# Own buffers for the merged branches, one more pair by seven products, and a reordered opening in a two-layer hybrid encoder

## The chip, the cores and the metric

The kernel runs on one core of one Trainium2 chip. The metric is the device time of one execution in microseconds (us). A core has five engines that run side by side and wait for one another through semaphores: TensorE (PE; its weight loads are listed apart as PEld), VectorE (DVE), ScalarE (ACT), GpSimd (POOL) and SyncE (SP). SP here only issues transfers; ACT and POOL issue a few too. Each engine takes its instructions strictly in the order in which they were laid down.

## What is computed

Two layers over 512 positions of width 1024. Each layer normalizes x, projects it, runs four token mixers side by side, gates and sums them, projects the sum back onto x, and then adds a gated feed-forward:

```python
for l in range(DEPTH):                        # DEPTH = 2
    h = rmsnorm(x, ln_mix[l])
    z = h @ w_in[l]
    (c_q, c_kv, k_rope, fnet_in, dq, dk, dv,
     hq, hi, hf_fwd, hf_bwd, hg, gate_logits) = split_cols(z, IN_WIDTHS)
    ...                                       # o_mla, o_fnet, o_diff, o_hgrn: 512 x 256 each
    merged = jnp.zeros_like(x)
    for n, o_branch in enumerate((o_mla, o_fnet, o_diff, o_hgrn)):
        gate = jax.nn.sigmoid(gate_logits[..., n * D_MODEL:(n + 1) * D_MODEL])
        merged = merged + gate * (o_branch @ w_branch[l, n])
    x = x + merged @ w_out[l]
    h2 = rmsnorm(x, ln_ffn[l])
    g_part, u_part = jnp.split(h2 @ w_gate_up[l], 2, axis=-1)
    x = x + (jax.nn.silu(g_part) * u_part) @ w_down[l]
```

D_MODEL is 1024 and the feed-forward is 2816 wide, which makes 22 blocks of 128.

## The kernel before

x is held transposed, as 8 tiles of 128 features by 512 positions (x[0] to x[7], 256 KB each). Every matrix operand is split into a rounded high part and a remainder: ACT writes the high part (L121, or L125 with a gain), DVE subtracts it to get the low part (L122, L126). A product of two such operands is three matmuls (`mm3`, L140 to L143). A `gemm` (L201) makes one 128 x 512 output tile from 8 blocks of 128, so from 24 matmuls. `weight` (L128) loads a 128 x 1024 block of weights over SP, and ACT and DVE split it; there are two raw buffers and three pairs of split ones (WR and WL, L30). Its instructions get a priority that moves them AHEAD = 156 places forward.

The order within each engine comes from a scheduler that works through the program by priority and puts a later instruction in front where an engine would otherwise stand idle by the scheduler's own idea of time. Buffers come from pools; a tile that reuses memory waits for the last reader of the tile that lay there.

**Opening of layer 0** (L77 to L98, L226 to L250). POOL builds the identity matrix, DVE fills `ones` and `blk64` with constants, ACT copies `blk64` (L86) and then loads the table for logarithm and exponential (L230) and issues the load of the small parameters `pk` (L231). SP issues the first quarter of the first weight block w_z[0], then x[0], the rest of that block, x[1] to x[7], and then the other weight blocks. `prenorm` (L168) multiplies each x[k] by its gain and splits it into hh[k] and hl[k], and adds up the squares of all eight tiles in `ss`. Four projections named hf00, hf01, hq0 and hg0 use this x that is not yet divided by its norm. `scale` (L186) sums `ss` over the partitions with a matmul by `ones` into `ssx` and makes the reciprocal root r; `normed` (L193) then writes hh and hl again, with r multiplied in. Everything later, first the projection `hi` (`gemm_tok`, L209), reads these.

**Mixers.** Five streams of work (HGRN, its projections, a chain of the others, gates and branches) are interleaved by a string written out by hand (ORDER, L34). The last mixer is `diff`, whose pool df is open from L852 until its generator ends. `branch` (L342) multiplies mixer output by w_branch and adds it, gated, to acc[nt]. `merged` (L371) scales each finished acc[k] by one half and splits it into mh[k] and ml[k]. These take the buffers of the tags hh and hl in pool hp, 8 of each, that hold the split x until then.

**Output projection** (L1009 to L1014). Eight gemms o0 to o7 over mh and ml; each result is added to x[nt]. Each of them reads all of mh and ml.

**Feed-forward** (L1020 to L1194). `prenorm` splits x again into hh and hl, in the same eight buffers. Three raw gemms fr0 to fr2 use it, with `scale` after the first, then `normed`. The 22 blocks are then made one pair (gate and up) at a time, as the string SEVEN says. `eight` (L1150) makes a pair by two ordinary gemms, 48 matmuls of 512 columns. `seven` (L1119) makes it by seven products of half-size blocks after Strassen and Winograd, 84 matmuls of 256 columns; two of the products are left to be run inside the next pair (`finish`, L1140). `sums` (L1069) loads what a pair by seven needs: the raw block, the wide block s31 of 1024 columns (a load over SP, and a second one from POOL that is added to it in flight), the block a22, two sums on DVE (s24), and five splits. It needs sums of x halves too, `right_sums` (L1041), which are made after pairs 0 to 3. SEVEN has six pairs by `eight` first, then 16 by `seven`. After 8, 16 and 22 pairs the down projection of these pairs is added to x.

Of the kernel before, what the change touches and what calls it, by code (L numbers as in the profile page):

```python
# [11 lines left out]
F32 = mybir.dt.float32  # L12
F32R = mybir.dt.float32r
# [6 lines left out]
P = 128  # L20
S = 512
NT = S // P
D = 1024
KD = D // P
# [4 lines left out]
LOG_EXP = "natural_log_exp_and_others"  # L29
WL, WR = 3, 2  # L30
LAYERS = range(L)
SEVEN = "8888887777777777777777"
AHEAD = 156
ORDER = "ccbccchhhchhcbchcghcchcchzccczccbccccccchgcgccchbbbcbhcgbzcbbcbccbgghcbgcgcbcccghchghchzhbccccbccccgcccccczhgcgbgchcgcccccccggggggbgcggggbcbbggcbbcbhcccbccbccccccccccccccccccbchccgbgggbchcbbbbbbhbbb"  # L34
PE = 8
PM = 4
# [10 lines left out]
PK_N = 416  # L47
# [15 lines left out]
def body(tc, io):  # L63
    nc = tc.nc
    V, A, T = nc.vector, nc.scalar, nc.tensor

    def pool(name, bufs=1, **kw):
        return tc.tile_pool(name=name, bufs=bufs, reuse_waits="tile", **kw)


    with pool("const") as cl, pool("hp") as hp, pool("wp", WL) as wp, pool("vals", side="right") as cp, \
# [2 lines left out]
            pool("pq", 2, space=bass.MemoryType.PSUM) as pq:  # L74


        ident = cl.tile([P, P], F32, name="ident")  # L77
        make_identity(nc, ident)
        ones = cl.tile([P, P], F32, name="ones")
        V.memset(ones, 1.0)  # L80
        blk64 = cp.tile([P, P], F32, name="blk64")
        V.memset(blk64, 0.0)
        V.memset(blk64[0:64, 0:64], 1.0)
# [5 lines left out]
        xpool = [None]  # L89
        x = []  # L90

        def load_x(src, who):
            xpool[0] = pool(f"x{who}", side="right")
            px = xpool[0].__enter__()
            x[:] = [px.tile([P, S], F32, name=f"x{who}_{k}") for k in range(KD)]
            return [lambda k=k: nc.sync.dma_start(x[k], src[k]) for k in range(KD)]

        def drop_x():  # L98
            xpool[0].__exit__(None, None, None)
# [5 lines left out]
        def acc_psum(name="g"):  # L105
            return pm.tile([P, S], F32, tag="mm", name=name)
# [10 lines left out]
        def add(out, a, b):  # L117
            V.tensor_tensor(out, a, b, op=ALU.add)  # L118

        def split(hi, lo, src):  # L120
            A.activation(hi, src, AF.Copy)  # L121
            V.tensor_tensor(lo, src, hi.bitcast(F32), op=ALU.subtract)  # L122

        def split_g(hi, lo, src, g):
            A.activation(hi, src, AF.Copy, scale=g)  # L125
            V.scalar_tensor_tensor(lo, src, g, hi.bitcast(F32), op0=ALU.mult, op1=ALU.subtract)  # L126

        def weight(src, n, name, cuts=(), between=None):  # L128
            raw = rp.tile([P, 1024], F32, tag="wr", name=f"wr_{name}")
            hi = wp.tile([P, 1024], F32R, tag="wh", name=f"wh_{name}")  # L130
            lo = wp.tile([P, 1024], F32R, tag="wl", name=f"wl_{name}")
            with tc.high_priority(AHEAD):
                for a, b in zip((0,) + cuts, cuts + (n,)):
                    nc.sync.dma_start(raw[:, a:b], src[:, a:b])
                    split(hi[:, a:b], lo[:, a:b], raw[:, a:b])
                    if between:
                        between.pop()()
            return hi, lo

        def mm3(ps, lh, ll, rh, rl, first, last):  # L140
            T.matmul(ps, lh, rh, start=first, stop=False)  # L141
            T.matmul(ps, lh, rl, start=False, stop=False)  # L142
            T.matmul(ps, ll, rh, start=False, stop=last)  # L143
# [57 lines left out]
        def gemm(w, hh, hl, name, ready=None):  # L201
            hi, lo = ready or weight(w, 1024, name)
            ps = acc_psum(name)
            for k in range(KD):
                c = slice(k * P, (k + 1) * P)
                mm3(ps, hi[:, c], lo[:, c], hh[k], hl[k], k == 0, k == KD - 1)
            return ps
# [18 lines left out]
        xs = nc.dram_tensor("x_mid", (KD, P, S), F32).ap()  # L226
        for l in LAYERS:
            lam_init = 0.8 - 0.6 * math.exp(-0.3 * l)
            pk = cp.tile([P, PK_N], F32, tag="pk", name=f"pk{l}")
            tc.keep_in_program_order(nc.scalar.preload_act_table_set(LOG_EXP))  # L230
            nc.scalar.dma_start(pk, io["pk"][l])  # L231


            if l == LAYERS[0]:
                with tc.high_priority(1000):
                    loads = load_x(io["x"], "in")
                    w0 = weight(io["w_z"][l, 0], 1024, "hf00", (256,), [loads[1], loads[0]])
                    for load in loads[2:]:
                        load()
            else:  # L240
                w0 = weight(io["w_z"][l, 0], 1024, "hf00")
            with pool(f"mo{l}") as mo, pool(f"mx{l}") as mp:
                hh, hl, scale, normed = prenorm(pk[:, PK_MIX:PK_MIX + 8], f"m{l}")
                first = [gemm(None, hh, hl, "hf00", w0)]
                r = scale()
                for c, name in ((1, "hf01"), (4, "hq0"), (6, "hg0")):
                    first.append(gemm(io["w_z"][l, c], hh, hl, name))
                sig0 = mp.tile([P, 3, S], F32, name="sig0")
                for j in range(2):
                    mul(sig0[:, j], first[j], r)  # L250
# [63 lines left out]
                done = set()  # L314
# [51 lines left out]
                        yield gate(n, nt)  # L366
                    done.add("gates")

                mh, ml = [], []

                def merged(n):  # L371
                    for k in range(len(mh), n):
                        h = hp.tile([P, S], F32R, tag="hh", name=f"mh{k}", bufs=KD)
                        lo = hp.tile([P, S], F32R, tag="hl", name=f"ml{k}", bufs=KD)
                        split_g(h, lo, acc[k], 0.5)
                        mh.append(h)
                        ml.append(lo)
# [472 lines left out]
                def diff():  # L850
                    yield 3
                    with pool(f"df{l}") as dp, ps_pool(f"dp{l}", 2) as dps:  # L852
# [112 lines left out]
                        for n, (i, t) in enumerate(units):  # L965
# [5 lines left out]
                            if t == NT - 1:  # L971
                                yield f"b{2 * KD - 1}"
                                yield from normed(i)
                        done.add(2)

                def chain(*gens):
                    for g in gens:
# [25 lines left out]
                for _ in hgrn_z(0):  # L1003
                    pass
                issue({"h": hgrn(), "z": hgrn_z(1), "c": chain(hgrn_v(), fnet(), mla(), diff()),
                       "g": gates(), "b": branches()}, ORDER)

# [4 lines left out]
                for nt in range(KD):  # L1012
                    ps = gemm(io["w_o"][l, nt], mh, ml, f"o{nt}", wo.get(nt))
                    add(x[nt], x[nt], ps)  # L1014

# [2 lines left out]
            with pool(f"fa{l}") as fa, pool(f"ff{l}") as fp, ps_pool(f"fr{l}", 2) as fr:  # L1020
                tc.keep_in_program_order(nc.scalar.preload_act_table_set(LOG_EXP))
                hh, hl, scale, _ = prenorm(pk[:, PK_FFN:PK_FFN + 8], f"f{l}")
# [46 lines left out]
                def sums(j):  # L1069
# [3 lines left out]
                    src = io["w_gu"][l, j]  # L1073
                    with tc.high_priority(AHEAD):
                        raw = rp.tile([P, 1024], F32, tag="wr", name=f"wr_f{j}")
# [97 lines left out]
                raw = []  # L1173
# [5 lines left out]
                for k0 in range(0, KF, 8):  # L1179
                    m = min(8, KF - k0)  # L1180
                    for j in range(k0, k0 + m):
                        (seven if SEVEN[j] == "7" else eight)(j)
                        if j < Q:
                            right_sums(j, r)
                    rest()
                    for nt in range(KD):
                        ps = acc_psum(f"d{nt}")
                        hi, lo = weight(io["w_d"][l, nt, :, k0 * P:(k0 + m) * P], m * P, f"d{nt}")
                        for j in range(m):
                            c = slice(j * P, (j + 1) * P)  # L1190
# [49 lines left out]
def layout(inp):  # L1240
# [9 lines left out]
    def tiles(a, n):  # L1250
# [18 lines left out]
    gu = gu.transpose(0, 2, 3, 1, 4).reshape(L, KF, P, 4, D // 2)  # L1269
    o["w_gu"] = np.stack([gu[:, j][:, :, [1, 0, 2, 3] if SEVEN[j] == "7" else [0, 1, 2, 3]]  # L1270
                          for j in range(KF)], 1).reshape(L, KF, P, 2 * D)
# [41 lines left out]
```

## Time and profile before

| | us |
|---|---|
| three runs | 1723.2, 1725.94, 1726.93 |
| median | 1725.94 |
| the profiled execution | 1724.95 |
| its span, first to last instruction | 1723.2 |
| what lies around the span | 1.75 |

| engine | busy us | share of the span |
|---|---|---|
| PE | 1697.8 | 99% |
| PEld | 1422.5 | 83% |
| DVE | 1179.0 | 68% |
| ACT | 808.8 | 47% |
| POOL | 43.0 | 2% |

In a row of the timeline stand the start, the time that the instruction took, engine, line and operation, the tile written and the tiles read, and in brackets how long the engine had stood idle and what ended that. A row of the chain of waits has start, time and what the time went to; there the time of a matmul is the step to the next one. A row of the busy time by stretch has, for each engine, the busy time and the number of instructions. A matmul of 512 columns is listed with 0.39 us though the next one starts 0.23 us later, since matmuls overlap, so a PE that is listed as busy may still be losing time.

### The profile page before, as it was taken

The numbers are of one execution on the slowest core, as the hardware profiler recorded it, in microseconds if no ns is written. First come the engines' busy times: TensorE is split into PE (matmuls) and PEld (weight loads), VectorE is DVE, ScalarE is ACT, GpSimd is POOL, SyncE is SP. The second block draws the span as 40 slices with busy tenths as digits, with TensorE's granted clock in tenths as the row PEclk, the third lists the DMA queues.
The fourth block names the chain that finished last, engine by engine and source line by source line (L and its number), as shares of the span: only waits on it lengthen the run. The fifth ranks groups of instructions, "written<-read, shape, count | busy, mean of one in ns | idle before, by whom it ended". The sixth has DMA issues, their size and how long they took to land.

```text
span 1723.2 us, 25722 instructions
## 1 busy us (share of the span) xinstructions
PE 1697.8 (99%) x10220; PEld 1422.5 (83%) x10220; DVE 1179.0 (68%) x1979; ACT 808.8 (47%) x1352; POOL 43.0 (2%) x68
## 2 busy tenths in 40 slices
PE   8999999999999999999999999999999999999999
PEld 6787778877787989989887777788777788899897
DVE  8858775457769647748677687754667695487473
ACT  7374353456555424525453743534564453254251
POOL 1000000000000000000000000000000000000000
PEclk9999999999999999999999999999999999999999
DMA  5222203332262435644442221142323624365443
GB/s 193 64 80 86 74 26 115 105 99 86 87 201 100 138 110 161 170 122 126 133 136 58 87 74 62 43 119 97 110 75 111 189 87 140 118 177 145 127 115 104
DMA packets 62473, 191.58 MB, mean 111 GB/s; under 512 B 7953, under 2 KB 9361, under 8 KB 62353
## 3 DMA queue, kind: packets, MB, share of 16 engines
q1 hardware_dynamic: 56304, 170.10, 30.4%
q0 software_dynamic: 5760, 19.42, 6.2%
q8 instruction: 80, 1.31, 0.3%
q10 hardware_dynamic: 288, 0.43, 0.1%
q14 instruction: 41, 0.33, 0.1%
HBM read 179.42 MB, written 4.19 MB: 107 GB/s over the span
## 4 chain that ended last, share of the span: by engine, by line
PE 87%; DVE 7%; ACT 3%; DMA 2%; issue 1%; SPq 0%; POOLq 0%; ACTq 0%; DVEq 0%
PE fb L1066 8%; PE g L142 6%; PE g L141 6%; PE g L143 6%; PE fc L1066 5%; PE fa L1066 5%; PE d L141 5%; PE d L143 5%; PE d L142 5%; PE f L142 3%; PE f L141 3%; PE f L143 3%; DMA s_f<-in_w_gu 2%; PE av L942 1%; PE sm L909 1%; PE hf L142 1%
## 5 line engine op out<-in xcount | busy, mean ns | idle before, releaser
L141 PE MATMUL g<-hhm,wh_g 128*128 128x512 f32 x512 | 202.0, 394 | 0.0
L143 PE MATMUL g<-hhm,wl_g 128*128 128x512 f32 x512 | 201.5, 394 | 0.0
L142 PE MATMUL g<-hlm,wh_g 128*128 128x512 f32 x512 | 201.5, 394 | 0.0
L143 PE MATMUL d<-ah,wl_d 128*128 128x512 f32 x352 | 136.9, 390 | 0.5 <-DVE wl_d L122 0.5
L141 PE MATMUL d<-ah,wh_d 128*128 128x512 f32 x352 | 137.2, 392 | 0.0
L142 PE MATMUL d<-al,wh_d 128*128 128x512 f32 x352 | 137.1, 390 | 0.0
L122 DVE TENSOR_TENSOR wl_g<-wr_g,wh_g 128x1024 fp32r<-128x1024 f32 x64 | 78.3, 1223 | 73.8 <-ACT wh_g L121 73.8
L121 ACT ACTIVATE wh_g<-wr_g 128x1024 fp32r<-128x1024 f32 x64 | 67.7, 1058 | 115.4 <-PE g L142 80.1
L142 PEld LDWEIGHTS g<-hlm,wh_g 128*128 128x128 f32 x512 | 96.3, 188 | 20.4 <-issue 1.5
L141 PEld LDWEIGHTS g<-hhm,wh_g 128*128 128x128 f32 x512 | 96.3, 188 | 20.2 <-issue 0.8
L143 PEld LDWEIGHTS g<-hhm,wl_g 128*128 128x128 f32 x512 | 96.3, 188 | 20.0 <-issue 0.8
L121 ACT ACTIVATE wh_d<-wr_d 128x1024 fp32r<-128x1024 f32 (+1 forms) x48 | 47.5, 989 | 111.7 <-PE d L142 85.5
L118 DVE TENSOR_TENSOR xm<-xm,d 128x512 f32<-128x512 f32 x48 | 33.0, 688 | 88.9 <-PE d L143 88.8
L121 ACT ACTIVATE wh_f<-wr_f 128x1024 fp32r<-128x1024 f32 x50 | 53.0, 1059 | 79.1 <-PE d L142 35.0
L121 ACT ACTIVATE vh_f<-s_f 128x512 fp32r<-128x512 f32 x64 | 40.1, 630 | 103.4 <-PE fb L1066 63.8
L910 DVE TENSOR_REDUCE nm<-sm 128x1 f32<-128x512 f32 x64 | 43.8, 689 | 51.3 <-PE sm L909 50.9
L143 PEld LDWEIGHTS d<-ah,wl_d 128*128 128x128 f32 x352 | 66.1, 188 | 14.9 <-DVE wl_d L122 1.4
L141 PEld LDWEIGHTS d<-ah,wh_d 128*128 128x128 f32 x352 | 66.0, 188 | 14.9 <-ACT ah L121 1.9
L142 PEld LDWEIGHTS d<-al,wh_d 128*128 128x128 f32 x352 | 66.1, 188 | 14.0 <-DVE al L122 1.2
L1066 PE MATMUL fb<-th,vh_f 128*128 128x256 f32 x256 | 75.7, 296 | 0.4 <-DVE uu L118 0.3
L1066 PE MATMUL fa<-hhf,wl_f 128*128 128x256 f32 x256 | 72.7, 284 | 0.0
L1066 PE MATMUL fa<-hlf,wh_f 128*128 128x256 f32 x256 | 72.5, 283 | 0.0
(444 smaller groups left out, 4845.6 us busy)
## 6 DMA issues: line engine op xcount, KB each, us to landing
wr_g<-in_w_g SPq DMA_DIRECT2D x64, 512.0 KB, 3.6
wr_f<-in_w_gu SPq DMA_DIRECT2D x50, 512.0 KB, 3.5
s_f<-in_w_gu SPq DMA_DIRECT2D x32, 512.0 KB, 4.5
s_f<-in_w_gu POOLq DMA_DIRECT2D x32, 512.0 KB, 5.4
wr_d<-in_w_d SPq DMA_DIRECT2D x32, 512.0 KB, 3.5
wr_b<-in_w_b SPq DMA_DIRECT2D x16, 512.0 KB, 3.4
wr_o<-in_w_o SPq DMA_DIRECT2D x16, 512.0 KB, 3.5
a_f<-in_w_gu SPq DMA_DIRECT2D x32, 256.0 KB, 3.0
```

Source lines behind the costliest of these rows:

```text
L118: V.tensor_tensor(out, a, b, op=ALU.add)
L121: A.activation(hi, src, AF.Copy)
L122: V.tensor_tensor(lo, src, hi.bitcast(F32), op=ALU.subtract)
L141: T.matmul(ps, lh, rh, start=first, stop=False)
L142: T.matmul(ps, lh, rl, start=False, stop=False)
L143: T.matmul(ps, ll, rh, start=False, stop=last)
L909: T.matmul(ps, qs[0:96, t * P:(t + 1) * P], ks[0:96], start=True, stop=True)
L910: V.tensor_reduce(nm[:, j:j + 1], ps, axis=AX.X, op=ALU.max, negate=True)
L942: T.matmul(av[e * 64:e * 64 + 64], vv[:, b, 2 * i + e], pts[i][e][:, b].rearrange("p t q -> p (t q)"), start=t == 1 and b == 0, stop=b == ...
L1066: T.matmul(ps[:, :H], lh[:, c], rh, start=first and k == 0 and n == 0, stop=k == Q - 1 and n == 2, skip_group_check=True)
```

## The change

1. **Merged branches.** mh and ml no longer reuse the tags hh and hl. They get 16 tiles in a pool of their own (om), opened when the first of them is written and closed after the output projection. For its memory to be free, diff's pool df is closed before diff reports that it is done.
2. **Feed-forward.** Since hh and hl are not held by mh and ml, the splits of the feed-forward's x[k] may be written while the output projection runs. SEVEN has five ordinary pairs instead of six, so pair 5 is made by seven products in each layer; the layout of its weights follows.
3. **Opening.** `pk` is loaded first of all, and the table for logarithm and exponential is loaded before ACT's first copy. `ones` is filled first, and PE runs ten matmuls of `ones` by `ones` (128 columns) into a PSUM tile that nobody reads. The second weight block, w_z[1], is loaded in two halves between the x tiles, and the order of the loads on SP is fixed: first quarter of w_z[0], x[0], rest of w_z[0], x[1] to x[3], first half of w_z[1], x[4] and x[5], second half, x[6] and x[7].

```diff
-SEVEN = "8888887777777777777777"
+SEVEN = "8888877777777777777777"
+EARLY = 10
...
+        pk0 = cp.tile([P, PK_N], F32, tag="pk", name=f"pk{LAYERS[0]}")
+        tc.keep_in_program_order(nc.scalar.dma_start(pk0, io["pk"][LAYERS[0]]))
+        tc.keep_in_program_order(nc.scalar.preload_act_table_set(LOG_EXP))
+        ones = cl.tile([P, P], F32, name="ones")
+        V.memset(ones, 1.0)
+
+        early = pq.tile([P, S], F32, tag="sc", name="early")
+        for _ in range(EARLY):
+            T.matmul(early[:, :P], ones, ones, start=True, stop=True)
         ident = cl.tile([P, P], F32, name="ident")
         make_identity(nc, ident)
-        ones = cl.tile([P, P], F32, name="ones")
-        V.memset(ones, 1.0)
...
-            pk = cp.tile([P, PK_N], F32, tag="pk", name=f"pk{l}")
-            tc.keep_in_program_order(nc.scalar.preload_act_table_set(LOG_EXP))
-            nc.scalar.dma_start(pk, io["pk"][l])
+            if l == LAYERS[0]:
+                pk = pk0
+            else:
+                pk = cp.tile([P, PK_N], F32, tag="pk", name=f"pk{l}")
+                tc.keep_in_program_order(nc.scalar.preload_act_table_set(LOG_EXP))
+                nc.scalar.dma_start(pk, io["pk"][l])
...
-                    loads = load_x(io["x"], "in")
-                    w0 = weight(io["w_z"][l, 0], 1024, "hf00", (256,), [loads[1], loads[0]])
-                    for load in loads[2:]:
-                        load()
+                    loads = load_x(io["x"], "in", tc.keep_in_program_order)
+                    some = lambda *ks: lambda: [loads[k]() for k in ks]
+                    w0 = weight(io["w_z"][l, 0], 1024, "hf00", (256,), [some(1, 2, 3), some(0)],
+                                tc.keep_in_program_order)
+                    w1 = weight(io["w_z"][l, 1], 1024, "hf01", (512,), [some(6, 7), some(4, 5)],
+                                tc.keep_in_program_order)
...
-                    first.append(gemm(io["w_z"][l, c], hh, hl, name))
+                    first.append(gemm(io["w_z"][l, c], hh, hl, name, w1 if c == 1 else None))
...
-                mh, ml = [], []
+                mh, ml, om = [], [], []
 
                 def merged(n):
+                    if not om:
+                        om.append(pool(f"om{l}"))
+                        om.append(om[0].__enter__())
                     for k in range(len(mh), n):
-                        h = hp.tile([P, S], F32R, tag="hh", name=f"mh{k}", bufs=KD)
-                        lo = hp.tile([P, S], F32R, tag="hl", name=f"ml{k}", bufs=KD)
+                        h = om[1].tile([P, S], F32R, name=f"mh{k}")
+                        lo = om[1].tile([P, S], F32R, name=f"ml{k}")
...
-                        done.add(2)
+                    done.add(2)
...
                     add(x[nt], x[nt], ps)
+                om[0].__exit__(None, None, None)
```

More of the change, by code (lines that the diff above doesn't have):

```diff
@@ L90, in body, with load_x @@
         x = []
-        def load_x(src, who):
+        def load_x(src, who, keep=lambda i: i):
             xpool[0] = pool(f"x{who}", side="right")
@@ L95, in load_x @@
             x[:] = [px.tile([P, S], F32, name=f"x{who}_{k}") for k in range(KD)]
-            return [lambda k=k: nc.sync.dma_start(x[k], src[k]) for k in range(KD)]
+            return [lambda k=k: keep(nc.sync.dma_start(x[k], src[k])) for k in range(KD)]
         def drop_x():
@@ L126, in split_g, with weight @@
             V.scalar_tensor_tensor(lo, src, g, hi.bitcast(F32), op0=ALU.mult, op1=ALU.subtract)
-        def weight(src, n, name, cuts=(), between=None):
+        def weight(src, n, name, cuts=(), between=None, keep=lambda i: i):
             raw = rp.tile([P, 1024], F32, tag="wr", name=f"wr_{name}")
@@ L133, in weight @@
                 for a, b in zip((0,) + cuts, cuts + (n,)):
-                    nc.sync.dma_start(raw[:, a:b], src[:, a:b])
+                    keep(nc.sync.dma_start(raw[:, a:b], src[:, a:b]))
                     split(hi[:, a:b], lo[:, a:b], raw[:, a:b])
@@ L228, in body @@
             lam_init = 0.8 - 0.6 * math.exp(-0.3 * l)
-            pk = cp.tile([P, PK_N], F32, tag="pk", name=f"pk{l}")
-            tc.keep_in_program_order(nc.scalar.preload_act_table_set(LOG_EXP))
-            nc.scalar.dma_start(pk, io["pk"][l])
+            if l == LAYERS[0]:
[4 more added lines that the diff above has]
+                nc.scalar.dma_start(pk, io["pk"][l])
             if l == LAYERS[0]:
                 with tc.high_priority(1000):
-                    loads = load_x(io["x"], "in")
-                    w0 = weight(io["w_z"][l, 0], 1024, "hf00", (256,), [loads[1], loads[0]])
-                    for load in loads[2:]:
-                        load()
+                    loads = load_x(io["x"], "in", tc.keep_in_program_order)
[4 more added lines that the diff above has]
+                                tc.keep_in_program_order)
             else:
+                w1 = None
                 w0 = weight(io["w_z"][l, 0], 1024, "hf00")
```

## The prediction, made before the changed kernel was run

> **What bounds the kernel now.** I read the page first, then PE's waits, then the chain of waits and the timeline at the three places that the change touches.
>
> ```profile
> span 1723.2 us, 25722 instructions
> ...
> PE 1697.8 (99%) x10220; PEld 1422.5 (83%) x10220; DVE 1179.0 (68%) x1979; ACT 808.8 (47%) x1352; POOL 43.0 (2%) x68
> ```
>
> PE is listed as busy for all but 25 us, so over the whole span PE sets the time, and a microsecond off PE's path is a microsecond off the kernel, unless another engine is late at the next place where PE needs it. What PE waited for (us in total, times, longest):
>
> ```profile
> PE hf L141 <- ACT hhm L125: 6.6, 1, 6.6
> ...
> PE fo L143 <- DVE ab L122: 1.9, 2, 1.0
> PE ssx L188 <- DVE ss L118: 1.2, 2, 0.7
> ```
>
> The largest wait is the opening, 6.6 us. Of the waits at places that the change touches there is one more, `ssx` in front of the feed-forward. The others, such as `fo`, lie inside the mixers, which the change leaves alone.
>
> The chain through the opening (start, time, what):
>
> ```profile
> 0.75 3.32 DMA wr_hf<-in_w_z
> ...
> 4.53 0.43 ACT L230
> 4.96 0.86 issue
> 5.82 0.73 ACT hhm L125
> ...
> 6.59 0.79 PE hf L141
> ...
> 12.77 0.43 PE hf L141
> ...
> 13.58 0.23 PE hf L143
> ```
>
> ACT's table load (L230) stands between the first weight split and the first x split. PE's steps are 0.43 us up to 12.77 and 0.23 from 13.58 on: the first 14 matmuls run at half speed, which costs 14 x 0.20 = 2.8 us. That is PE's side. Whether it counts is decided by DVE, which makes the low parts:
>
> ```profile
> 0.85 0.17 DVE L80 MEMSET ones<- 128x128 f32 x1 [0.85 <-PEq L1298]
> ...
> 1.19 0.42 SPq L96 DMA_DIRECT2D xin<-in_x  x1
> ...
> 6.58 0.75 DVE L126 SCALAR_TENSOR_TENSOR hlm<-xin,pk,hhm 128x512 fp32r<-128x512 f32 x1 [1.14 <-ACT hhm L125]
> ...
> 20.10 0.42 DVE L115 TENSOR_TENSOR rotm<-trig,pk 128x256 f32<-128x256 f32 x1
> ...
> 33.11 0.69 ACT L121 ACTIVATE wh_hi<-wr_hi 128x576 fp32r<-128x576 f32 x1 [1.23 <-PE hg L142]
> ...
> 33.83 0.76 DVE L122 TENSOR_TENSOR wl_hi<-wr_hi,wh_hi 128x576 fp32r<-128x576 f32 x1 [0.78 <-ACT wh_hi L121]
> ...
> 37.17 0.40 PE L221 MATMUL hi<-wh_hi,hhm 128*128 128x288 f32 x1 [0.61 <-ACT hhm L121]
> ...
> 111.17 0.39 PE L567 MATMUL hb<-ql,ss 128*128 128x128 f32 x2
> ```
>
> ```profile
> DMA to landing us min/median/max: 3.7/5.3/5.9
> ```
>
> ```profile
> 6.58:20.20 13.62, 13.61 (x43) 9.92 (x44) 13.49 (x25) 12.28 (x22) 0.00 (x0) 1.00 0.70 247
> 20.20:33.10 12.90, 12.90 (x56) 10.37 (x56) 11.89 (x21) 8.61 (x12) 3.25 (x6) 1.00 0.63 183
> 33.10:42.20 9.10, 8.49 (x62) 8.11 (x61) 8.34 (x14) 5.91 (x10) 0.00 (x0) 1.00 0.37 114
> ```
>
> In the stretches (us, then busy time and count of PE, PEld, DVE, ACT, POOL) DVE works 13.49 of 13.62, 11.89 of 12.90 and 8.34 of 9.10 us, from its first x split to the last normed one. When `hi` meets the third block of normed x at 37.17, PE has waited 0.61 us for it. So PE was already ahead of DVE there, and the opening is worth what DVE gains, not what PE gains.
>
> **The change part by part.** *Opening.* With the table loaded during the 3.32 us in which nothing has landed, the load at 4.53 goes. The trace has no switch cost beside it: it begins at 4.53, and x[0] is split at 5.82, 1.29 later. The Trainium skill (ScalarE: Activation LUTs, What ACT_TABLE_LOAD costs) agrees on 1283 ns but adds a drain of 1380 ns to each switch; no drain shows here, and by its figure the sum would be the same, because the landing of x[0] is the next limit. x[0] is issued at 1.19; the shortest landing of the eight is 3.7, which I take for x[0] since it is nearly first in the queue, so it is there at 4.9. (Bounds: it may land as late as 5.82, which gains nothing.) ACT and DVE start 5.82 - 4.9 = 0.92 us earlier.
>
> The second gain of DVE is in its wait of 0.78 at 33.83. It goes back to ACT, which waited for `hg`, PE's last raw gemm, to free a buffer pair. PE comes earlier by more than that, so the wait goes. PE's lead: 0.92 from the start, up to 2.8 from the clock, which ten matmuls on `ones` (filled at 0.85 to 1.02) keep busy from about 1 us on, and some from the second weight block, which is there between x[3] and x[4], so that PE has hf01's first half to do while x[4] to x[7] land. A lead of 0.93 is enough (DVE's 1.54 below less the 0.61), and I see about 4.
>
> The costs. Splitting w_z[1] in halves gives DVE two instructions of 128 x 512 for one of 128 x 1024:
>
> ```profile
> L122 DVE TENSOR_TENSOR wl_g<-wr_g,wh_g 128x1024 fp32r<-128x1024 f32 x64 | 78.3, 1223 | 73.8 <-ACT wh_g L121 73.8
> ...
> L118 DVE TENSOR_TENSOR xm<-xm,d 128x512 f32<-128x512 f32 x48 | 33.0, 688 | 88.9 <-PE d L143 88.8
> ```
>
> that is 2 x 0.69 - 1.22 = 0.16. The 512 KB put ahead of x[4] to x[7] delay x[7] and, with it, the sum of squares, but DVE has all of the other splits to do meanwhile; it is the busy engine, so I take nothing (bound: at 247 GB/s, the mean of that first stretch, 2.1 us later). `pk` moves ahead of the table load on ACT's queue and lands no later. The early matmuls could hold PE back: a 128-column matmul in plain float32 is a pair of instructions like that at 111.17, 0.39 us at full clock, so ten take at most 7.8 us at half clock and end by 8.8. With the clock up, hf00's 24 steps of 0.23 would then end at 14.3; now they end at 13.58 + 10 x 0.23 = 15.9, so PE leads all the same. In this trace the clock needed 7 us of work (6.59 to 13.58); then it is up at about 8. The Trainium skill (TensorE: Matmul & The Clock Gate, Part 1) says about 4 us, a window of 3.4 us that runs freely; that would be 5. The sum is the same by either, since DVE decides.
>
> Opening: 0.92 + 0.78 - 0.16 = 1.54. Bounds: -0.5 (no earlier x[0], later x[7]) and 0.92 + 1.9 + 1.5 = 4.3 (all of DVE's idle time in the three stretches, 0.13 + 1.01 + 0.76, and four products for the rotary tables, like the one at 20.10, pushed behind, 1.5).
>
> *Output projection to feed-forward.* The rows are of both layers for `ssx`, of layer 0 for the rest:
>
> ```profile
> 499.13 1.15 ACT L121 ACTIVATE vh_f<-s_f 128x512 fp32r<-128x512 f32 x2 [7.40 <-DMA s_f<-in_w_gu]
> ...
> 509.47 4.06 DVE L126 SCALAR_TENSOR_TENSOR hlf<-xm,pk,hhf 128x512 fp32r<-128x512 f32 x6
> ...
> 516.50 1.49 DVE L118 TENSOR_TENSOR ss<-ss,sq 128x512 f32<-128x512 f32 x2
> ...
> 518.05 1.13 PE L188 MATMUL ssx<-ss,ones 128*128 128x512 f32 x2 [0.57 <-DVE ss L118]
> ...
> 524.47 1.06 ACT L121 ACTIVATE wh_f<-wr_f 128x1024 fp32r<-128x1024 f32 x1 [3.90 <-PE fr L142]
> ...
> 1372.11 1.12 PE L188 MATMUL ssx<-ss,ones 128*128 128x512 f32 x2 [0.68 <-DVE ss L118]
> ```
>
> ACT stood 7.40 us at 499.13 waiting for the prefetched wide block of the first seven-product pair, and DVE behind it. Then six x splits come in a row at 509.47, because each buffer hh[k] still held mh[k] until o7 had read it. The last two sums of squares are done at 518.0, so PE waits 0.57 for them, and 0.68 in layer 1. With own buffers the splits of x[0] to x[6] follow their additions, and behind o7 there are left one addition, one split, one square and one sum, under 3 us against the 5.4 us (24 x 0.227) of fr0. Gain 0.57 + 0.68 = 1.25. Cover: if the splits still come late, it is 0. What is late next is the normed splits, which move up with `ssx`.
>
> The pool om lies in memory that the feed-forward's pools use next, and its tiles are read until o7 ends. If the wide block shares it, its load waits for o7 and ACT's wait moves behind it (a rival, below). Opening om costs nothing: the last reads of diff's tiles lie ahead of branch 2, whose result mh needs.
>
> *The sixth pair.* Two rows of an ordinary pair, 48 matmuls apart, and two of successive seven-product pairs:
>
> ```profile
> 563.07 0.39 PE L141 MATMUL f<-hhf,wh_f 128*128 128x512 f32 x1
> ...
> 573.95 0.39 PE L141 MATMUL f<-hhf,wh_f 128*128 128x512 f32 x1
> ...
> 664.18 0.39 PE L1066 MATMUL fb<-th,vh_f 128*128 128x256 f32 x1 [0.32 <-DVE uu L118]
> ...
> 674.62 0.38 PE L1066 MATMUL fb<-th,vh_f 128*128 128x256 f32 x1
> ```
>
> 573.95 - 563.07 = 10.88 for an ordinary pair; 674.62 - 664.18 = 10.44 for the other, 0.3 of it a wait for `uu`. Gain 0.44 in each layer, 0.88. (At best the 84 steps run through, 10.44 - 0.32 = 10.12, and it is 1.5.) The pair now begins 10.9 us earlier, near 568.5, and brings DVE sums and splits. DVE's room:
>
> ```profile
> 530.00:541.00 11.00, 10.95 (x48) 8.53 (x47) 10.86 (x17) 5.40 (x8) 0.00 (x0) 1.00 0.13 48
> ...
> 563.00:574.00 11.00, 11.00 (x51) 9.10 (x50) 8.65 (x27) 5.76 (x9) 0.87 (x1) 1.00 0.46 162
> 574.00:579.40 5.40, 5.40 (x26) 4.46 (x25) 2.61 (x3) 2.96 (x4) 0.00 (x0) 1.00 0.59 97
> ```
>
> It is full from 530 to 541 (10.86 of 11) and has 2.35 + 2.79 = 5.1 us in the 16.4 ahead of the present first such pair. The added work, a wide split of 1.22, two sums and three splits of 0.69, less two ordinary splits of 1.22, is 2.2. I take no stall (bound: 2.2 in each layer).
>
> Sum: 1.54 + 1.25 + 0.88 = 3.67. The profiled execution took 1724.95, so 1721.3 for one like it; the median of the runs, 1725.94, lies 0.99 higher, so I forecast 1722.3.
>
> **The rivals.** *The x split does not move.* ACT's wait of 7.40 came from the prefetch, not from the buffers; if the prefetch still sits among the additions, the sums of squares stay late, and the 1.25 is not gained: 1723.5. For it: the wait is in order on ACT, and DVE's additions came behind it. Against: six splits in a row at 509.47, which only the buffers explain.
>
> *DVE gains more at the opening.* The scheduler fills the idle 1.9 us and puts the rotary products behind: 4.3 instead of 1.54, so 1719.5. For it: the raw gemms end some 4 us earlier, and every wait of ACT on them goes. Against: the order on DVE was full already.
>
> *Slower: the wide block's wait moves behind o7.* If its load must wait for om, ACT waits in order where it makes the root and the normed splits. The row at 524.47 shows 3.90 us of idle time on ACT there; 7.40 - 3.90 = 3.5 is left, and DVE, 10.86 of 11, can't make it good. In two layers that is 7.0, and `ssx` gains nothing: 1725.94 - 1.54 - 0.88 + 7.0 = 1730.5. It decides once the wait is over 6.8 us (3.9 plus half of 2.42 + 3.45). Against: a load that waits is laid down later by the scheduler too, and there are 50 us until the pair.
>
> *The clock falls again.* PE, 4 us early, then idles for DVE around `hi`, and if the clock drops, another 14 slow steps cost 2.8 us: 1725.1. For it, only a rule: the Trainium skill (TensorE: Matmul & The Clock Gate, Part 1) has the clock halved after an idle window of about 3.4 us. Against: after PE's idle spells in this trace (the longest past the opening is 1.0) no step of 0.43 follows, and here it would idle in pieces.
>
> **How the numbers follow.** A measurement of this kernel can tell 0.2%, 3.45 us, from no change; the bound is 1722.5. Chances: forecast 0.50 (its own range 1721 to 1723.5, a little over half below the bound), no x split 0.18, more at the opening 0.21, slower 0.06, clock 0.05. Faster: 0.29 + 0.21 = 0.50. Same: 0.21 + 0.18 + 0.05 = 0.44. Slower 0.06. The range goes from 1718.9 (more at the opening, and the pairs at their best) to 1726.1 (no x split, nothing at the opening, and a stall of 0.5 in each layer).
>
> **What would show it.** Right: ACT with its table load ahead of the first weight split and the first x split near 4.9; PE's steps at 0.23 by about 8; DVE without its gap ahead of the third `wl_hi`, and the normed block that `hi` met at 37.17 there about 1.5 us earlier; x splits between the additions along o1 to o7, and no wait at `ssx`; 10.4 us for each of 17 pairs. Wrong: a wait of PE in front of `ssx` or inside the first seven-product pair, an ACT wait for `s_f` behind o7, PE waiting over 3 us at `hi` and stepping at 0.43 after it, or that block more than 3 us early.

## The result, and the profile after

The changed kernel takes 1734.21 us (median of four runs, 1732.49 to 1738.03), the kernel before 1724.86 beside it (four runs, 1723.20 to 1726.93, the three shown above among them). The ratio is 1.0057, 95% interval 1.0036 to 1.0078: slower by 0.57%, and outside the forecast range. The profiled execution took 1734.42 us, and its span is 9.4 us longer than before:

```profile
span 1732.6 us, 25936 instructions
...
PE 1704.6 (98%) x10312; PEld 1430.4 (83%) x10312; DVE 1188.4 (69%) x2000; ACT 812.3 (47%) x1362; POOL 44.3 (3%) x70
```

From PE's waits (us in total, times, longest):

```profile
PE f L149 <- ACT hhf L129: 5.7, 3, 2.7
...
PE f L150 <- DVE hlf L130: 2.3, 4, 1.0
...
PE hf L149 <- ACT hhm L133: 1.4, 1, 1.4
```

The two rows of `f` are new: before, PE had no wait worth listing in the ordinary pairs. The wait at `ssx` is gone from the list, as forecast. The opening's 6.6 is now 1.4, but mostly because the ten matmuls that nobody reads fill it: PE's first useful step moved only from 6.59 to 5.42. So the change did what was claimed at the output projection and part of it at the opening, and something else happened at the start of the feed-forward. There, in layer 0 (start, length, engine, line, what; idle time before it in brackets):

```profile
507.00 0.71 ACT L133 ACTIVATE hhf<-xm,pk 128x512 fp32r<-128x512 f32 x1
...
508.38 0.33 SPq L142 DMA_DIRECT2D wr_f<-in_w_gu  x1
...
511.28 0.39 PE L151 MATMUL o<-mh,wl_o 128*128 128x512 f32 x1
...
511.47 0.33 SPq L1097 DMA_DIRECT2D s_f<-in_w_gu  x1
...
511.50 0.39 PE L149 MATMUL fr<-hhf,wh_fr 128*128 128x512 f32 x1
...
516.61 0.89 POOL L1100 DMA_DIRECT2D s_f<-in_w_gu  x1 [287.74 <-PE fr L151]
...
518.00 0.69 ACT L158 ACTIVATE y<-ssx,eps 128x512 f32<-128x512 f32 x1
...
525.30 0.63 ACT L129 ACTIVATE vh_f<-s_f 128x512 fp32r<-128x512 f32 x1 [6.61 <-DMA s_f<-in_w_gu]
...
525.84 0.62 ACT L159 ACTIVATE y<-y 128x512 f32<-128x512 f32 x1
...
528.38 0.63 ACT L129 ACTIVATE vh_f<-s_f 128x512 fp32r<-128x512 f32 x1 [0.88 <-DMA s_f<-in_w_gu]
...
530.54 0.63 ACT L129 ACTIVATE hhf<-xn 128x512 fp32r<-128x512 f32 x1 [0.59 <-DVE xn L1053]
...
531.23 0.65 PE L149 MATMUL f<-hhf,wh_f 128*128 128x512 f32 x1 [2.33 <-ACT hhf L129]
...
573.76 0.28 PE L1085 MATMUL fa<-hhf,wh_f 128*128 128x256 f32 x1
```

Read it from the top. The x split at 507.00 lies between the additions of the output projection; that part worked. SP sends the load of the wide block `s_f` at 511.47, at the last product of o7 (511.28). The waits of SP's own queue name that product as what the load waited for, 3.0 us in each layer:

```profile
SPq L1097 <- PE o L151: 5.9, 2, 3.0
```

Before, the split of this block stood at 499.13, along the output projection. Now POOL adds the second half at 516.61, and both are in place only at 525.30. In ACT's order the narrow split of this block (`vh_f`) stands between the two halves of the reciprocal root: the Ln is at 518.00, and the Exp, which depends on nothing but the Ln, at 525.84. After it come three more narrow splits, two of the same block and one of the second wide block with a second wait of 0.88, and a weight split. The first normed split starts at 530.54.

ACT takes its instructions strictly in order here: the Exp was ready at 518.69 and waited 7.15 us behind a split that nobody needed for another 48 us. The Trainium skill (TensorE: Matmul & The Clock Gate, the specs and "Engine queue depths") says the same: PE can pull weight loads ahead in its queue, while ScalarE's and VectorE's queues are strictly first in, first out.

The same places before:

```profile
511.87 0.39 PE L141 MATMUL fr<-hhf,wh_fr 128*128 128x512 f32 x1
...
525.43 0.61 ACT L121 ACTIVATE hhf<-xn 128x512 fp32r<-128x512 f32 x1
...
579.39 0.28 PE L1066 MATMUL fa<-hhf,wh_f 128*128 128x256 f32 x1
```

From `fr`'s first step to the first step of `fa` it was 579.39 - 511.87 = 67.52 us, with twelve ordinary gemms of 24 x 0.2269 = 5.446: 2.17 more than these need. Now it is 573.76 - 511.50 = 62.26 with ten: 7.80 more. Layer 1 has 2.35 and 7.76. This extra time, which I call the loss of the stretch, is the measure for all that follows. The two layers lose 15.56 - 4.52 = 11.04 us more than before. With the two pairs at the forecast -0.88 and everything up to the end of layer 0's output projection 0.37 earlier, the sum is +9.8; the span grew by 9.4. The loss is not all idle time: it holds the product `ssx` itself, about 1.0 in each layer, and steps that are slow at a low clock.

How the engines stood (window, its length, busy time and count of PE, PEld, DVE, ACT, POOL, granted clock, DMA share, GB/s):

```profile
520.00:530.00 10.00, 8.89 (x40) 7.03 (x38) 4.00 (x7) 3.77 (x6) 0.87 (x1) 1.00 0.65 149
530.00:540.00 10.00, 7.55 (x20) 5.12 (x21) 10.00 (x15) 6.65 (x9) 0.00 (x0) 0.66 0.35 124
```

PE is idle for 1.1 and 2.4 us, and the granted clock falls to 0.66. DVE has 4.00 of 10 us to do in the first window and is full in the second: it waits for the Exp, and then everything comes at once.

The opening:

```profile
4.64 0.72 ACT L133 ACTIVATE hhm<-xin,pk 128x512 fp32r<-128x512 f32 x1 [0.55 <-DMA xin<-in_x]
...
6.79 0.84 ACT L129 ACTIVATE wh_hf<-wr_hf 128x768 fp32r<-128x768 f32 x1 [0.80 <-DMA wr_hf<-in_w_z]
...
8.39 0.49 PE L149 MATMUL hf<-hhm,wh_hf 128*128 128x512 f32 x1 [1.45 <-ACT hhm L133]
...
20.85 0.68 DVE L126 TENSOR_TENSOR ss<-ss,sq 128x512 f32<-128x512 f32 x1
...
22.56 0.59 PE L196 MATMUL ssx<-ss,ones 128*128 128x512 f32 x1
...
25.00 0.69 DVE L160 SCALAR_TENSOR_TENSOR ya<-ssx,y 128x512 f32<-128x512 f32 x1 [1.30 <-ACT y L159]
...
41.52 0.68 DVE L130 TENSOR_TENSOR hlm<-xn,hhm 128x512 fp32r<-128x512 f32 x1
```

The first x split moved from 5.82 to 4.64, as the prediction had it, and the gap ahead of the third `wl_hi` is gone. But the rest of the first weight block lands only for 6.79, PE waits 1.45 at 8.39, and later the order on DVE turns against it: a weight's low part and a rotary product now stand ahead of the last sum of squares (20.85; before 19.34), `ssx` comes at 22.56 instead of 20.24, and DVE waits 1.30 for the root at 25.00. Nor did the early matmuls keep the clock up: they end at 5.70, PE's useful steps come with gaps for data from 5.42 on, the granted clock is 0.50 from 10 to 12, and they take 0.43 again up to 12.49. They take 0.23 only from 12.77 on (before: from 13.41). The last low part of the normed x starts at 41.52. Before, it started at 41.49.

### The profile page after: what moved, and what is told of

Same layout as the page of the kernel before. It is cut to its first block, busy times and chain, and to the rows that moved or that the text cites. A ratio compares the mean times of both kernels' runs of the same rounds, so it can differ in the third digit from the quotient of the medians.

```text
span 1732.6 us, 25936 instructions
## 1 busy us (share of the span) xinstructions
PE 1704.6 (98%) x10312; PEld 1430.4 (83%) x10312; DVE 1188.4 (69%) x2000; ACT 812.3 (47%) x1362; POOL 44.3 (3%) x70
## 3 DMA queue, kind: packets, MB, share of 16 engines
q8 instruction: 81, 1.33, 0.3%
## 4 chain that ended last, share of the span: by engine, by line
PE 85%; DVE 8%; ACT 3%; DMA 2%; issue 1%; SPq 0%; POOLq 0%; ACTq 0%; DVEq 0%
PE fb L1085 9%; PE g L150 6%; PE g L149 6%; PE g L151 6%; PE fc L1085 6%; PE fa L1085 5%; PE d L151 5%; PE d L149 5%; PE d L150 5%; PE f L150 2%; PE f L149 2%; PE f L151 2%; PE o L150 2%; PE o L151 2%; PE o L149 2%; DMA s_f<-in_w_gu 1%
## 5 line engine op out<-in xcount | busy, mean ns | idle before, releaser
L1085 PE MATMUL fb<-th,vh_f 128*128 128x256 f32 x272 | 80.2, 295 | 0.2
L1085 PE MATMUL fa<-hhf,wl_f 128*128 128x256 f32 x272 | 77.2, 284 | 0.0
L1085 PE MATMUL fa<-hlf,wh_f 128*128 128x256 f32 x272 | 77.0, 283 | 0.0
```

The lines of the kernel that those rows point to most:

```text
L1085: T.matmul(ps[:, :H], lh[:, c], rh, start=first and k == 0 and n == 0, stop=k == Q - 1 and n == 2, skip_group_check=True)
```

## The experiments

Two theories for the 11. *Queue*: the wide block is loaded late because of the merged branches' own pool, and its split stands in ACT's order ahead of the normed splits. *Room*: the seven-product pair that is brought forward overfills DVE and ACT. Each time is followed by its ratio to the kernel before, run beside it, with the 95% interval.

**e2_six.** Only the number of ordinary pairs goes back.

```diff
-SEVEN = "8888877777777777777777"
+SEVEN = "8888887777777777777777"
```

> The changed kernel with six ordinary pairs first again; merged branches in their own buffers and the new opening stay. Accounts common to all: opening -0.4, no wait at ssx -1.25, sixth pair -0.88, so the feed-forward's start must cost about 12.0 in the two layers (6.2 and 5.8). Queue theory: the wide block is loaded late because the pool of merged branches is given back only when o7 has read it, and ACT, in order, stands at its split between the two halves of the reciprocal root. With six ordinary pairs the block's slot lies 2 KB higher, off the last merged tile, but in SP's queue it still stands behind the fourth ordinary weight block, which went out at 508.4; so it goes out near 508.8 in place of 511.5, ACT's wait of 6.6 shrinks to about 4, and the time is 1724.9 - 0.4 - 1.25 + 12.0 - 2 x 2.7 = 1729.8. Room theory (the pair brought forward by 10.9 us overfills DVE and ACT at 530 to 570): the 12.0 goes with the pair, 1723.2, and ACT has no long wait for s_f behind o7.

1735.26 us, 1.0063 (1.0050 to 1.0076). The room theory falls: without the earlier pair the stall is whole. The load did go out 2.7 earlier against `fr` (509.97 here), without waiting for o7:

```profile
507.23 0.42 SPq L1097 DMA_DIRECT2D s_f<-in_w_gu  x1
...
512.85 0.89 POOL L1100 DMA_DIRECT2D s_f<-in_w_gu  x1 [285.48 <-DMA a_f<-in_w_gu]
...
523.29 0.63 ACT L129 ACTIVATE vh_f<-s_f 128x512 fp32r<-128x512 f32 x1 [6.14 <-DMA s_f<-in_w_gu]
...
528.54 0.63 ACT L129 ACTIVATE hhf<-xn 128x512 fp32r<-128x512 f32 x1 [0.16 <-DVE xn L1053]
```

But it brought only 0.5: from POOL's issue to ACT's split it took 10.44 us, in the changed kernel 8.69. My 1729.8 took the landing to move with the issue. So the slot that the block shares with the last merged tile accounts for 2.7 us of the load's delay and no more. Here SP's queue shows no wait of its own for `s_f`: the load goes out right behind the ordinary weight block of 506.85, so it is its place in SP's order that makes it late.

**e3_shared.** The merged branches go back into the x splits' buffers; the rest of the change stays.

```diff
-                        h = om[1].tile([P, S], F32R, name=f"mh{k}")
+                        h = hp.tile([P, S], F32R, tag="hh", name=f"mh{k}", bufs=KD)
```

(and the same for the low part, with the pool `om` taken out).

> The changed kernel with the merged branches back in the x splits' buffers; five ordinary pairs first and the new opening stay. Queue theory: the wide block goes out near 483 again, ACT waits for it along the output projection (about 7 us, near 499), the x splits come in a row behind o7, PE waits 0.6 at ssx in each layer, and the feed-forward starts without a stall: 1724.9 - 0.4 - 0.88 = 1723.6. Room theory: the stall stays, 1724.9 - 0.4 - 0.88 + 12.0 = 1735.6.

1722.99 us, 0.9989 (0.9981 to 0.9998). The stall is gone, and with it the late load:

```profile
480.46 0.38 SPq L1093 DMA_DIRECT2D s_f<-in_w_gu  x1
```

**e4_opening.** e3_shared with six ordinary pairs, so the opening alone.

> Only the new opening: merged branches in the x splits' buffers, six ordinary pairs first. Both theories: the accounts of the opening, -0.4, so 1724.5. Should the opening be the cost (a clock that is lower over the whole run after it), it would come out at 1730 or more.

1724.40 us, 0.9998 (0.9989 to 1.0007). As expected; the opening is no cost, and its gain too small to be measured.

**e5_behind.** The whole change; only the order on ACT is mended. The narrow splits of the first wide blocks are issued behind the last normed split.

```diff
                 def normed(r):
                     for k in range(KD):
-                        split(hh[k], hl[k], gained(k, r))
+                        last[0] = split(hh[k], hl[k], gained(k, r)).ins
...
-                        v1 = pair(s31[:, 512:], 512)
-                        v3 = pair(s31[:, :512], 512)
-                        v22 = pair(a22, 512)
+                        with tc.issue_after(last[0]):
+                            v1 = pair(s31[:, 512:], 512)
+                            v3 = pair(s31[:, :512], 512)
+                            v22 = pair(a22, 512)
```

> The whole change, and the narrow splits of the first wide blocks (vh_f, vl_f) queued on ACT behind the last normed split; loads and memory untouched. Queue theory: the load still goes out at about 511.5, but Ln and Exp follow each other near 518, the normed splits start near 525 or before, PE has no wait of 2.3 at the first ordinary product and steps at 0.23 there: 1724.9 - 0.4 - 1.25 - 0.88 = 1722.3. A rival to it, that the late load itself is the cost: PE waits in the first seven-product pair instead, and no more than half of the 12.0 comes back, 1728 or more. Room theory: 1734, as the changed kernel.

1722.50 us, 0.9988 (0.9979 to 0.9997). The load is as late as in the changed kernel (512.64 in this execution), and it no longer matters:

```profile
519.18 0.69 ACT L159 ACTIVATE y<-ssx,eps 128x512 f32<-128x512 f32 x1
...
519.90 0.63 ACT L160 ACTIVATE y<-y 128x512 f32<-128x512 f32 x1
...
525.40 0.61 ACT L129 ACTIVATE hhf<-xn 128x512 fp32r<-128x512 f32 x1
...
538.04 0.62 ACT L129 ACTIVATE vh_f<-s_f 128x512 fp32r<-128x512 f32 x1
```

Exp follows Ln at once, the normed splits begin 12.72 us after `fr` (512.68), and the wide block's split has its turn at 538.04. The second window from above, here:

```profile
530.00:540.00 10.00, 9.95 (x44) 7.72 (x43) 10.00 (x16) 5.74 (x10) 0.00 (x0) 1.00 0.17 60
```

This shows the cause: the edit touches nothing but the place of these narrow splits (each is a copy on ACT and a subtraction on DVE), the load went out as late against `fr` as in the changed kernel, and 11.7 us came back.

**e7_late.** The opposite way: the kernel before, with the two first wide blocks' loads queued behind the fourth ordinary weight block.

```diff
-                        nc.sync.dma_start(s31, src[:, 512:1536])
+                        with tc.issue_after(sent["f3"]) if j < 8 else tc.high_priority(0):
+                            nc.sync.dma_start(s31, src[:, 512:1536])
```

> The kernel before, with one thing changed: the loads of the first two wide blocks are queued on SP behind the load of the fourth ordinary feed-forward block; buffers, opening and pairs as before. Its ACT order then has the wide block's split between the two halves of the root, as in the changed kernel. Queue theory: a late load and that order are all it takes, about 6 us in each layer, 1724.8 + 12 = 1737 (1735 to 1738), with an ACT wait for s_f of 5 to 8 us behind Ln near 525. Rival, that the own buffers or the earlier pair are needed for it: 1725 to 1728.

1731.46 us, 1.0046 (1.0032 to 1.0060). A late load alone makes the kernel slower, without own buffers and without an earlier pair, but by 6.8, not 12. The expectation missed the order too: ACT's wait lies ahead of Ln, not between the two halves of the root:

```profile
509.18 0.42 SPq L1080 DMA_DIRECT2D s_f<-in_w_gu  x1
...
521.41 0.63 ACT L122 ACTIVATE vh_f<-s_f 128x512 fp32r<-128x512 f32 x1 [6.79 <-DMA s_f<-in_w_gu]
...
522.90 0.67 ACT L151 ACTIVATE y<-ssx,eps 128x512 f32<-128x512 f32 x1
...
523.99 0.62 ACT L152 ACTIVATE y<-y 128x512 f32<-128x512 f32 x1
...
528.75 0.63 ACT L122 ACTIVATE hhf<-xn 128x512 fp32r<-128x512 f32 x1 [2.14 <-DVE xn L1035]
```

The landing took 7.0 from POOL (514.45), so ACT is free 9.49 after `fr`'s first step (511.92), 4.3 earlier than in the changed kernel, and the normed splits come at 528.75.

**e10_alone** and **e11_f4** were to test a line through these kernels, from the end of ACT's wait to the loss. e10_alone is the changed kernel with the second wide block's loads behind `wr_f6`; e11_f4 is e7_late one weight block later (`sent["f4"]`).

> The changed kernel, with the loads of the second wide block (s_f and a_f of the pair after) queued on SP behind two more ordinary weight blocks, so that the first block's accumulating transfer has less beside it. Theory: that transfer took 8.7 from POOL's issue to ACT's split in the changed kernel, 10.4 in e2_six and 7.0 in e7_late because it shares the DMA engines with the second block; alone it takes about 7, so ACT's wait ends near 523.6, 12.1 after o7 in place of 13.8. The three kernels with a stall give a line: 3.4 us in each layer for a split 9.5 after o7's end, 6.2 for 13.8, so 0.65 for each us: 5.1 here, 1734.2 - 2 x 1.1 = 1732.0. Rival, that the transfer's time doesn't come from sharing: 8.7 again, 1734.2.

1742.30 us, 1.0097 (1.0081 to 1.0112):

```profile
515.78 0.89 POOL L1103 DMA_DIRECT2D s_f<-in_w_gu  x1 [287.52 <-PE fr L152]
...
522.51 0.63 ACT L130 ACTIVATE vh_f<-s_f 128x512 fp32r<-128x512 f32 x1 [4.54 <-DMA s_f<-in_w_gu]
...
543.14 0.63 ACT L130 ACTIVATE vh_f<-s_f 128x512 fp32r<-128x512 f32 x1 [6.22 <-DMA s_f<-in_w_gu]
```

The part on the transfer holds: without the second block's loads beside it, it took 6.73 from POOL's issue to the split, and 5.70 in layer 1. The time does not. The second block's split kept its place among the normed splits, and now ACT waits there, 6.22 at 543.14: a new wait in order, of the same kind.

> The kernel before with the loads of the first two wide blocks queued on SP behind the fifth ordinary feed-forward block, one later than in e7_late. ACT's order then has Ln and Exp together and the wide block's first split behind them, ahead of all normed splits. Theory, that the end of ACT's wait sets the stall wherever on the way to the normed splits it lies: load out near 515, split near 527 to 528.5, 15.5 to 16.5 after o7, by the line 7.3 to 8 us in each layer, 1739.5 to 1741. Rival, that the place inside the root makes the stall: 2 us or less in each layer, 1729 or less.

1734.34 us, 1.0055 (1.0042 to 1.0067):

```profile
520.32 0.63 ACT L152 ACTIVATE y<-y 128x512 f32<-128x512 f32 x1
...
528.83 0.63 ACT L122 ACTIVATE vh_f<-s_f 128x512 fp32r<-128x512 f32 x1 [7.87 <-DMA s_f<-in_w_gu]
...
530.31 0.61 ACT L122 ACTIVATE hhf<-xn 128x512 fp32r<-128x512 f32 x1
```

Both expectations fail. ACT's wait ends 15.73 after `fr` (513.10), later than in the changed kernel, but the layers lose 3.1 and 4.6 us more than before, neither 7.3 to 8 nor under 2; with the root done, the first normed split follows 1.5 behind the wait, not 5.2. What counts is not when the wait ends but when the first normed split starts. The kernels by that measure (layer 0 / layer 1, us after `fr`'s first step, from the timelines):

```
kernel       wide split      first normed split   loss of the stretch
before       ahead of fr     13.56 / 13.75         2.17 / 2.35
e3_shared    ahead of fr     13.92 / 13.37         2.53 / 1.97
e4_opening   ahead of fr     14.27 / 12.91         2.85 / 1.49
e5_behind    25.36 / 25.37   12.72 / 12.73         1.33 / 1.33
e7_late       9.49 /  9.25   16.83 / 16.58         5.35 / 5.06
e11_f4       15.73 / 16.87   17.21 / 18.35         5.23 / 6.95
e2_six       13.32 / 12.98   18.57 / 18.50         7.50 / 6.93
changed      13.80 / 12.95   19.04 / 19.38         7.80 / 7.76
e10_alone    11.72 / 10.64   16.96 / 15.89        12.11 / 10.21
```

The loss is the start of the first normed split less 11.4, within 0.6 in every row but e10_alone's, which has the second wait. In the rows with a stall, one us later at that split is one us on the kernel. The rows without a stall lie on the same line for another reason: PE's waits there (0.57 in layer 0 before, 0.66 in e3_shared, none in e5_behind) are ahead of `ssx`, and they put off the split and the stretch alike.

**e6_noearly, e9_oldopen, e8_four** are e5_behind with one more thing changed: without the ten early matmuls; with the opening of before; with four ordinary pairs.

> The mended kernel (e5_behind) without the ten early matmuls of ones. If they lift the clock sooner: first steps of 0.23 later than in e5_behind and its like (11 to 13), near 16, and 1.5 to 2 us more, 1724.3. If they do nothing for it, as the steps of 0.43 after them suggest: 1722.5 and the rise where it was.

1722.66 us, 0.9990 (0.9981 to 0.9998): no difference in time. `hg` began at 28.13 there. A second profile of it:

> A second profile of e6_noearly. In seven profiles of kernels with the early matmuls of ones the raw gemm hg began at 25.73 to 27.51, in four with the opening of before at 27.69 to 27.77, in the one without early matmuls at 28.13. If the early matmuls are what brings it forward, hg begins at 27.7 or later here again; if that was chance, below 27.5.

1723.45 us in one run beside 1725.30 for the kernel before. `hg` began at 27.06, the side that the expectation calls chance: 28.13 and 27.06 without early matmuls overlap with 25.71 to 27.51 in eight profiles with them. What they are worth stays open.

> The mended kernel with the opening of before: own buffers, five ordinary pairs, splits behind the last normed split. By the accounts 1724.8 - 1.25 - 0.88 = 1722.6 to 1722.9, 0.4 over e5_behind; by the prediction's 1.54 for the opening, 1724.0.

1723.13 us, 0.9993 (0.9984 to 1.0001): 0.6 over e5_behind, inside the intervals.

> The mended kernel with four ordinary pairs first, one seven-product pair more. By the rows of the pairs 0.88 less, 1721.6. Rival: DVE is full from 530 to 552 and the fourth block of right sums is due at once, so PE waits in the first seven-product pair, 2 us or more in each layer, 1726.

1737.48 us, 1.0076 (1.0063 to 1.0088). The stretch up to the first seven-product pair is untouched (loss 1.34), but inside the pair PE waits for weight splits and for the right sums (`th`, `tl`), while DVE, on which both depend, is full from 530 to 560:

```profile
PE fb L1086 <- ACT wh_f L129: 4.1, 2, 2.1
PE fc L1086 <- ACT th L129: 3.5, 2, 1.8
...
PE fc L1086 <- DVE tl L130: 1.8, 2, 0.9
```

```profile
560.00:570.00 10.00, 5.10 (x23) 4.20 (x23) 9.26 (x28) 5.66 (x8) 0.86 (x1) 0.80 0.38 111
```

PE is busy 5.10 of 10 us. Room is a real limit, one pair further on. This is the room theory's mechanism, with the fourth block of right sums due at once. The kernel takes 15.0 us more than e5_behind; the three waits make up 9.4 of it, and the clock is lower there too (0.80).

> A second profile of e5_behind: no wait for s_f on ACT ahead of the normed splits, PE at 0.23 a step in the first ordinary pairs; hg again between 25.7 and 27.5; whether the clock drops at 64 to 71 again is open (it did in e4_opening, e5_behind and e11_f4, not in the others).

The second profile of e5_behind: 1722.13 us in one run, as expected. `hg` began at 25.71, and the clock did drop, at 63 to 70 (below).

## Why the prediction was wrong, point by point

**The side was wrong, by a rival that I had named.** "The wide block's wait moves behind o7" is what happened. I gave it 0.06 and a price of 3.5 us in each layer, and the loss grew by 5.6 and 5.4. Two steps of it failed.

*The chance.* I argued that "a load that waits is laid down later by the scheduler too, and there are 50 us until the pair". The load was laid down later, behind the weight block of 508.38. The split was not moved far enough: it stands ahead of the Exp. Presumably the scheduler held the block to be there by then; its own times are not on record. That 48 us were left until the pair needed it made no difference, since in a queue the instructions behind it count, and behind it stood the root. e5_behind shows it: with that order mended the same late load costs nothing. In the changed kernel the load waits for o7; why it stands behind that weight block in SP's order, in e2_six too, was not traced further. With the merged branches in the x splits' buffers it went out at 480.46.

*The price.* I took 7.40 of wait less 3.90 of ACT's idle time. But that idle time lay between the Exp and the first normed split, where DVE finishes the root: most of it is part of the chain and no slack. From the Exp to that split it took 5.50 before (519.93 to 525.43) and 4.70 after (525.84 to 530.54), so 0.80 was covered, not 3.90. What has to be priced is the start of the first normed split: 13.56 after `fr` before, 19.04 now.

**The x split moves: right, and its gain was larger than the 1.25.** Splits between the additions, no wait at `ssx`. With the order mended the loss is 1.33 in each layer, against 2.17 and 2.35: 1.86 in all by the profile. In time the own buffers are worth 0.5 (e5_behind against e3_shared), not told apart from nothing.

**The sixth pair: right in kind.** 0.88 was forecast; e3_shared less e4_opening is -1.4, with intervals of about 1.5 on each, so the size is not shown. I took "no stall", and PE's waits in all seven-product pairs together are 0.2 in e3_shared and 0.7 in e5_behind. e8_four shows that one pair more would have broken it.

**The opening: the x split's 0.92 held (it moved 1.18), the sum of 1.54 did not.** The step that failed is DVE's: its gap of 0.78 went, as predicted, but another wait took its place, 1.30 at 25.00, for a root whose sum of squares had been moved back in DVE's order. The last normed low part started 0.03 later than before. The sign "PE's steps at 0.23 by about 8" failed as well (12.77): the prediction counted on the ten matmuls to bring the clock up, and took nothing for the gaps behind them. In time the opening is worth 0.4 (e4_opening) or 0.6 (e9_oldopen against e5_behind), neither told apart from nothing.

**"The clock falls again": it fell, elsewhere and at no price that shows.** The granted clock was 0.66 at 530 to 540, where I had looked at `hi`. In e2_six's layer 1 and in both layers of e7_late it stayed at 1.00 through the same stretch, and the losses lie on the same line within its 0.6. DVE is full in that window, so PE may have had time to be slow; no run tests that.

Without the stall the number would have come out: 1722.3 was forecast, and e5_behind gives 1722.50. That they meet so closely is in part luck. The forecast started from a median of 1725.94, and beside e5_behind the kernel before took 1724.77: a gain of 3.64 was forecast, and 2.27 was measured (0.5 to 3.6), with less at the opening. e5_behind beats the kernel before by 0.12% (0.03 to 0.21%), little more than can be told apart, and the changed kernel by 11.7 us.

## What to carry to other kernels

A prefetch that waits costs what stands behind its consumer in that engine's order, not what the consumer is needed for: look up the queue, and price the start of the first instruction of the main chain behind it. If a scheduler lays out the order by times of its own, tie work with slack behind the chain by hand (the narrow splits of two blocks here, 11.7 us) sooner than put off other loads, which only moved the wait (e10_alone). Where the load can go out early again, as in e3_shared, that does as well: 1722.99 against 1722.50 is no difference that these intervals can tell. And idle time of an engine inside a chain of two engines is little cover.

## What the runs showed of the hardware

**The clock drops without a long wait, and not every time.** Two executions with the same instructions at 64 to 72, with waits of PE of 0.34 at 61.4 and 0.31 at 64.6 in e5_behind (window, length, busy times, clock):

```profile
64.00:68.00 4.00, 3.69 (x46) 3.25 (x45) 4.00 (x10) 0.60 (x1) 0.00 (x0) 0.60 0.10 38
68.00:72.00 4.00, 4.00 (x44) 3.51 (x45) 2.85 (x7) 0.39 (x1) 0.00 (x0) 0.55 0.00 0
```

and 0.35 and 0.30 in the changed kernel:

```profile
64.00:68.00 4.00, 3.31 (x50) 2.45 (x48) 4.00 (x10) 0.98 (x2) 0.00 (x0) 1.00 0.18 72
68.00:72.00 4.00, 3.37 (x47) 2.68 (x47) 4.00 (x10) 0.00 (x0) 0.00 (x0) 1.00 0.00 0
```

In the first the clock is at half from about 65 to 71, and the output projection starts 1.2 us later than in the other (468.20 and 467.02; at 59.5 the two were 0.02 apart). In the second it stays up. That PE is idle for longer there follows from its faster steps and explains nothing; from 60 to 64, ahead of the drop, PE was busy alike in both (1.66 and 1.99 us of 2 against 1.65 and 1.99). Products of 64 x 64 and 128 x 128 are at work. Five of fourteen profiles of this case showed the drop (e4_opening, e5_behind, e11_f4, e12_noearly, e13_behind). The Trainium skill (TensorE: Matmul & The Clock Gate, Part 1) has the clock halved after an idle window of about 3.4 us, and calls the window free-running, so that the same kernel differs from run to run. The second part fits these runs; an idle window is not to be seen in them. What sets off the drop stays open.

**An accumulating load's time depends on what runs beside it.** From POOL's issue to the split that waits for it, the same transfer took 6.73 and 5.70 us (layer 0 and 1) in e10_alone, with the second block's loads put off, and 8.69 and 7.99 in the changed kernel, which differs in nothing else. It took 7.0 and 6.8 in e7_late, and 10.4 and 9.8 in e2_six, where the second block's loads had been sent just ahead.
